# Loads and stores of a grouped softmax on two rings, the stores issued by ScalarE three tiles behind the loads

## The chip, the cores and the metric

The kernel runs on one core of a Trainium2 chip. The metric is device time in microseconds (us) of one execution. All runs that are compared here were with a granted clock of 1.0. A core has 16 transfer engines, which move all data between HBM (the large memory, where input and output lie) and SBUF (the memory that the compute engines work in). Of the compute engines this kernel needs VectorE (DVE in the profile) and ScalarE (ACT). SyncE (SP) and ScalarE can each issue transfers into a queue of their own; such a queue is called a ring here.

## The reference

```python
def reference(x):                      # x: 4 x 4096 x 4352, float32
    B, N, D = x.shape
    x_g = x.reshape(B, N, 8, D // 8)   # softmax over groups of 544
    x_g = x_g - x_g.max(axis=-1, keepdims=True)
    exp = np.exp(x_g)
    out = exp / exp.sum(axis=-1, keepdims=True)
    return out.reshape(B, N, D)
```

285 MB go in and 285 MB come out, and the arithmetic on an element is short.

## The kernel before

A tile has 256 rows of the input, two on each of 128 partitions: 34,816 bytes per partition, 4.456 MB. There are 64 tiles and six buffers. VectorE takes the negated maximum of a row, ScalarE the exponential with that maximum as bias (and the sum on the way), VectorE the reciprocal and the scaling in place. SyncE issues every transfer in one fixed order, on one ring:

```python
    with nc.Block(no_gpsimd_drain=True) as block:      # inner block
        @block.sync
        def _(sync):
            def load(t):
                b = t % NT                             # NT = 6 buffers
                if t >= NT:
                    sync.wait_ge(stored[b], 16 * (t // NT))
                sync.dma_start(out=bufs[b][:, :], in_=xt[t]).then_inc(landed[b], 16)
            for t in range(NT - 1):
                load(t)
            for t in range(nt):                        # nt = 64 tiles
                sync.wait_ge(scaled, R * (t + 1))      # R = 2 rows a tile
                sync.dma_start(out=ot[t], in_=bufs[t % NT][:, :]).then_inc(stored[t % NT], 16)
                if t + NT - 1 < nt:
                    load(t + NT - 1)
            # ... waits for the last stores
        # ... VectorE and ScalarE: hardware loops over 12 rows, VectorE one maximum ahead
```

Of the kernel before, what the change touches and what calls it, by code (L numbers as in the profile page):

```python
# [1 line left out]

# [5 lines left out]


@with_exitstack  # L10
def kernel(
    ctx: ExitStack,
    tc: tile.TileContext,
    x: bass.AP,
    out: bass.AP,
):
    nc = tc.nc
    G = 8
    P = 128
    R = 2  # L20
    NT = 6
    S = R * NT
    xf = x.flatten_outer_dims()
    of = out.flatten_outer_dims()
    N, D = xf.shape
    Dg = D // G
    nt = N // (P * R)
    nr = nt * R
    turns = (nr - 1) // S
    f32 = mybir.dt.float32  # L30
    X = mybir.AxisListType.X
    Exp = mybir.ActivationFunctionType.Exp
    xt = xf.rearrange("(t p r) d -> t p (r d)", p=P, r=R)
    ot = of.rearrange("(t p r) d -> t p (r d)", p=P, r=R)

    ctx.enter_context(tc.tile_critical(no_gpsimd_drain=True))  # L36
    ctx.enter_context(nc.cleanup_on_exit())
    bufs = [ctx.enter_context(nc.sbuf_tensor(f"xt{b}", [P, R * D], f32)) for b in range(NT)]
    mx = ctx.enter_context(nc.sbuf_tensor("mx", [P, S, G], f32))
    sm = ctx.enter_context(nc.sbuf_tensor("sm", [P, S, G], f32))  # L40
    rs = ctx.enter_context(nc.sbuf_tensor("rs", [P, S, G], f32))
    landed = [nc.alloc_semaphore(f"landed{b}") for b in range(NT)]
    stored = [nc.alloc_semaphore(f"stored{b}") for b in range(NT)]
    max_done = nc.alloc_semaphore("max_done")
    exp_done = nc.alloc_semaphore("exp_done")
    rec_done = nc.alloc_semaphore("rec_done")
    scaled = nc.alloc_semaphore("scaled")

    def row(s):
        b, r = divmod(s, R)  # L50
        return bufs[b][:, r * D:(r + 1) * D].rearrange("p (g d) -> p g d", g=G)

    def vector_max(s):
        if s % R == 0:
            nc.vector.sem_inc(landed[s // R], -16).wait_op(landed[s // R], 16, "sem-ge")  # L55
        nc.vector.reduce_max(out=mx[:, s, :], in_=row(s), axis=X, negate=True).then_inc(max_done, 1)  # L56

    def vector_scale(s):
        nc.vector.sem_inc(exp_done, -1).wait_op(exp_done, 1, "sem-ge")  # L59
        nc.vector.reciprocal(out=rs[:, s, :], in_=sm[:, s, :]).then_inc(rec_done, 1)  # L60
        nc.vector.sem_inc(rec_done, -1).wait_op(rec_done, 1, "sem-ge")  # L61
        xr = row(s)
        for g in range(G):
            i = nc.vector.tensor_scalar_mul(  # L64
                out=xr[:, g, :], in0=xr[:, g, :], scalar1=rs[:, s, g:g + 1])
        i.then_inc(scaled, 1)

    def scalar_exp(s):
        nc.scalar.sem_inc(max_done, -1).wait_op(max_done, 1, "sem-ge")  # L69
        xr = row(s)  # L70
        for g in range(G):
            i = nc.scalar.activation(  # L72
                out=xr[:, g, :],
                in_=xr[:, g, :],
                func=Exp,
                bias=mx[:, s, g:g + 1],
                scale=1.0,
                accum_out=sm[:, s, g:g + 1],
            )
        i.then_inc(exp_done, 1)  # L80

    def loop(engine):

        return nc.Fori(
            0, turns, engines=OrderedEngineSet([engine.engine]), head_slot={engine.engine: 0})

    with nc.Block(no_gpsimd_drain=True) as block:  # L87


        @block.sync  # L90
        def _(sync):
            def load(t):
                b = t % NT
                if t >= NT:
                    sync.wait_ge(stored[b], 16 * (t // NT))
                sync.dma_start(out=bufs[b][:, :], in_=xt[t]).then_inc(landed[b], 16)

            for t in range(NT - 1):
                load(t)
            for t in range(nt):  # L100
                sync.wait_ge(scaled, R * (t + 1))
                sync.dma_start(out=ot[t], in_=bufs[t % NT][:, :]).then_inc(stored[t % NT], 16)
                if t + NT - 1 < nt:
                    load(t + NT - 1)
            for b in range(NT):
                sync.wait_ge(stored[b], 16 * ((nt - b + NT - 1) // NT))


        @block.vector
        def _(vector):  # L110
            vector_max(0)
            with loop(vector):
                for s in range(S):
                    vector_max((s + 1) % S)
                    vector_scale(s)
            for n in range(turns * S, nr):
                if n + 1 < nr:
                    vector_max((n + 1) % S)
                vector_scale(n % S)

        @block.scalar
        def _(scalar):
            scalar.preload_act_table(Exp)  # L123
            with loop(scalar):
                for s in range(S):
                    scalar_exp(s)
            for n in range(turns * S, nr):
                scalar_exp(n % S)


# [1 line left out]
_INS = ['x']  # L132
_OUTS = [((4, 4096, 4352), 'float32')]


# [23 lines left out]
```

## Time and profile before

| | before |
|---|---|
| time, median (range, runs) | 1330.49 us (1329.97 to 1331.25, 4) |
| span in the trace | 1328.7 us |
| VectorE, ScalarE busy | 78%, 58% |
| bytes, mean rate over the span | 570.5 MB, 429 GB/s |
| last landing of a store, from the start | 1326.24 us |
| from there to the end of the span | 2.47 us |

The rows to start from are those of the transfers: a kernel whose 16 transfer engines are full in 39 of 40 slices has little to win elsewhere. The prediction below shows these rows and how they were read. Two more stretches of the kernel before are needed later. The columns of the row of a stretch are: stretch and its length, busy time of VectorE, ScalarE and GpSimd with the number of instructions, the granted clock, the busy share of the transfer engines, and GB/s.

```profile
64.00:66.00 2.00, 2.00 (x1) 0.68 (x2) 0.00 (x0) 1.00 1.21 522
66.00:76.00 10.00, 9.70 (x14) 6.76 (x19) 0.00 (x0) 1.00 1.00 428
76.00:80.00 4.00, 4.00 (x8) 4.00 (x12) 0.00 (x0) 1.00 1.01 435
80.00:100.00 20.00, 19.61 (x22) 13.16 (x37) 0.00 (x0) 1.00 0.98 422
...
1290.00:1300.00 10.00, 5.14 (x13) 3.99 (x12) 0.00 (x0) 1.00 1.02 439
```

There is no gap while the pipeline fills (a packet, here one row of 34,816 bytes, counts wholly where it starts, so that a short stretch can show more than 1.00), and none at 1290 to 1300 us, where the changed kernel will show one.

### The profile page before, as it was taken

What the parts mean: (1) busy time and instruction counts of PE and PEld (TensorE: products, weight loads), DVE (VectorE), ACT (ScalarE), POOL (GpSimd) and SP (SyncE); (2) the same over time, 40 slices, a digit from 0 to 9 for tenths busy, and PEclk for the clock granted to TensorE, in tenths of its full rate; (3) what the DMA queues carried; (4) which work ended last, traced back from release to release, by engine and by line L of the source; (5) the groups of instructions that cost most, each with busy time, mean ns of one, the idle gap of its engine ahead of it and who ended that gap; (6) DMA issues with size and microseconds to landing.
All of it is one profiled execution on the core that took longest, in us unless ns stands there. A gap on an engine that the chain in (4) does not pass through costs nothing. (4 is left out here: it accounts for less than half of the span.)

```text
span 1328.7 us, 4036 instructions
## 1 busy us (share of the span) xinstructions
DVE 1041.5 (78%) x1280; ACT 764.4 (58%) x2049; POOL 0.2 (0%) x4
## 2 busy tenths in 40 slices
DVE  5999987787877878778778787787877877878770
ACT  3777765655656556555565565655655556556560
POOL 0000000000000000000000000000000000000000
DMA  9999999999999999999999999999999999999997
GB/s 401 418 434 434 434 430 428 432 436 433 435 433 431 429 436 434 436 435 430 429 436 434 435 435 432 428 435 435 434 436 434 429 431 436 434 435 434 431 430 336
DMA packets 18441, 570.51 MB, mean 429 GB/s; under 512 B 2048, under 2 KB 2048, under 8 KB 2048
## 3 DMA queue, kind: packets, MB, share of 16 engines
q1 hardware_dynamic: 18432, 570.43, 99.6%
q14 instruction: 9, 0.07, 0.0%
HBM read 285.21 MB, written 285.21 MB: 429 GB/s over the span
## 5 line engine op out<-in xcount | busy, mean ns | idle before, releaser
L72 ACT ACTIVATE xt<-xt,mx 128x544 f32<-128x544 f32 x1024 | 751.3, 735 | 528.7 <-ACTq L69 528.7
L56 DVE TENSOR_REDUCE mx<-xt 128x8 f32<-128x4352 f32 x128 | 599.1, 4680 | 234.0 <-DVEq L55 233.1
L64 DVE TENSOR_SCALAR xt<-xt,rs 128x544 f32<-128x544 f32 x1024 | 434.0, 497 | 19.2 <-DVEq L61 0.9
L72 ACT ACTIVATION_READ_ACCUMULATOR xt<-xt,mx 128x1 f32 x1024 | 191.1, 187 | 0.0
L60 DVE RECIPROCAL rs<-sm 128x8 f32<-128x8 f32 x128 | 24.5, 191 | 3.2 <-DVEq L59 3.2
L123 ACT ACT_TABLE_LOAD x1 | 1.3, 1283 | 0.9 <-SPq L36 0.9
L143 POOL MEMSET const-bfloat16-1.0<- 128x1 bf16 x1 | 0.1, 102 | 0.0
L143 POOL MEMSET const-uint8-127<- 128x1 uint8 x1 | 0.1, 102 | 0.0
L143 POOL MEMSET const-float32-0.0<- 128x1 f32 x1 | 0.1, 99 | 0.2 <-issue 0.2
L143 POOL MEMSET const-float32-1.0<- 128x1 f32 x1 | 0.1, 99 | 0.0
## 6 DMA issues: line engine op xcount, KB each, us to landing
xt<-in_x_dram SPq DMA_DIRECT2D x64, 4352.0 KB, 30.8
out_dram<-xt SPq DMA_DIRECT2D x64, 4352.0 KB, 40.7
```

The source lines that it names most:

```text
L56: nc.vector.reduce_max(out=mx[:, s, :], in_=row(s), axis=X, negate=True).then_inc(max_done, 1)
L60: nc.vector.reciprocal(out=rs[:, s, :], in_=sm[:, s, :]).then_inc(rec_done, 1)
L64: i = nc.vector.tensor_scalar_mul(out=xr[:, g, :], in0=xr[:, g, :], scalar1=rs[:, s, g:g + 1])
L72: i = nc.scalar.activation(out=xr[:, g, :], in_=xr[:, g, :], func=Exp, bias=mx[:, s, g:g + 1], scale=1.0, accum_out=sm[:, s, g:g + 1],)
L123: scalar.preload_act_table(Exp)
L143: nc = _bacc.Bacc("TRN2", target_bir_lowering=False, num_devices=1)
```

## The change

Its intent: give loads and stores a ring each, so that neither is stuck behind the other in one queue; take the issue of stores from SyncE to ScalarE, inside its hardware loop; keep the distance steady by issuing the store of tile t only when the load of tile t + 3 has been seen; and drop the inner block with its barrier and cleanup.

```diff
+    LAG = 3
-    ctx.enter_context(nc.cleanup_on_exit())
...
+    def store(b, target):
+        take(nc.scalar, scaled, R)
+        nc.scalar.dma_start(out=target, in_=bufs[b][:, :]).then_inc(stored[b], 16)
+    def scalar_tile(j, target=None):
+        take(nc.scalar, seen)            # VectorE adds 1 when load j has landed
+        if target is not None:
+            store((j - LAG) % NT, target)
+        for r in range(R):
+            scalar_exp(j * R + r)
-    with nc.Block(no_gpsimd_drain=True) as block:
...
+    for t in range(nt):                  # SyncE: loads only
+        b = t % NT
+        if t >= NT:
+            nc.sync.wait_ge(stored[b], 16 * (t // NT))
+        nc.sync.dma_start(out=bufs[b][:, :], in_=xt[t]).then_inc(landed[b], 16)
...
+    for j in range(LAG):
+        scalar_tile(j)
+    with loop(nc.scalar) as u:
+        for b in range(NT):
+            scalar_tile(LAG + b, turn_out[u, b])
+    for j in range(rest, nt):
+        scalar_tile(j, ot[j - LAG])
+    for t in range(nt - LAG, nt):
+        store(t % NT, ot[t])
```

(`take` waits for a semaphore and counts it down. The arithmetic on both engines is unchanged.)

More of the change, by code (lines that the diff above doesn't have):

```diff
@@ L27 @@
     nt = N // (P * R)
-    nr = nt * R
-    turns = (nr - 1) // S
+    turns = (nt - LAG) // NT
+    rest = LAG + turns * NT
     f32 = mybir.dt.float32
@@ L34 @@
     ot = of.rearrange("(t p r) d -> t p (r d)", p=P, r=R)
+    turn_out = of[:turns * S * P, :].rearrange("(u b p r) d -> u b p (r d)", b=NT, p=P, r=R)
+    landed = [tc.alloc_semaphore(f"landed{b}") for b in range(NT)]
+    stored = [tc.alloc_semaphore(f"stored{b}") for b in range(NT)]
+    seen = tc.alloc_semaphore("seen")
+    max_done = tc.alloc_semaphore("max_done")
+    exp_done = tc.alloc_semaphore("exp_done")
+    rec_done = tc.alloc_semaphore("rec_done")
+    scaled = tc.alloc_semaphore("scaled")
     ctx.enter_context(tc.tile_critical(no_gpsimd_drain=True))
-    ctx.enter_context(nc.cleanup_on_exit())
     bufs = [ctx.enter_context(nc.sbuf_tensor(f"xt{b}", [P, R * D], f32)) for b in range(NT)]
@@ L41, with loop, take @@
     rs = ctx.enter_context(nc.sbuf_tensor("rs", [P, S, G], f32))
-    landed = [nc.alloc_semaphore(f"landed{b}") for b in range(NT)]
-    stored = [nc.alloc_semaphore(f"stored{b}") for b in range(NT)]
-    max_done = nc.alloc_semaphore("max_done")
-    exp_done = nc.alloc_semaphore("exp_done")
-    rec_done = nc.alloc_semaphore("rec_done")
-    scaled = nc.alloc_semaphore("scaled")
+    def loop(engine):
+        return nc.Fori(
+            0, turns, engines=OrderedEngineSet([engine.engine]), head_slot={engine.engine: 0})
+    def take(engine, sem, n=1):
+        engine.sem_inc(sem, -n).wait_op(sem, n, "sem-ge")
     def row(s):
@@ L51, in row, with vector_max, vector_scale @@
         return bufs[b][:, r * D:(r + 1) * D].rearrange("p (g d) -> p g d", g=G)
-    def vector_max(s):
+    def vector_max(n):
+        s = n % S
         if s % R == 0:
-            nc.vector.sem_inc(landed[s // R], -16).wait_op(landed[s // R], 16, "sem-ge")
+            take(nc.vector, landed[s // R], 16)
+            nc.vector.sem_inc(seen, 1)
         nc.vector.reduce_max(out=mx[:, s, :], in_=row(s), axis=X, negate=True).then_inc(max_done, 1)
-    def vector_scale(s):
-        nc.vector.sem_inc(exp_done, -1).wait_op(exp_done, 1, "sem-ge")
+    def vector_scale(n):
+        s = n % S
+        take(nc.vector, exp_done)
         nc.vector.reciprocal(out=rs[:, s, :], in_=sm[:, s, :]).then_inc(rec_done, 1)
-        nc.vector.sem_inc(rec_done, -1).wait_op(rec_done, 1, "sem-ge")
+        take(nc.vector, rec_done)
         xr = row(s)
@@ L66, in vector_scale, with scalar_exp @@
         i.then_inc(scaled, 1)
-    def scalar_exp(s):
-        nc.scalar.sem_inc(max_done, -1).wait_op(max_done, 1, "sem-ge")
+    def scalar_exp(n):
+        s = n % S
+        take(nc.scalar, max_done)
         xr = row(s)
@@ L80, in scalar_exp @@
         i.then_inc(exp_done, 1)
-    def loop(engine):
-        return nc.Fori(
-            0, turns, engines=OrderedEngineSet([engine.engine]), head_slot={engine.engine: 0})
-    with nc.Block(no_gpsimd_drain=True) as block:
-        @block.sync
-        def _(sync):
-            def load(t):
-                b = t % NT
-                if t >= NT:
-                    sync.wait_ge(stored[b], 16 * (t // NT))
-                sync.dma_start(out=bufs[b][:, :], in_=xt[t]).then_inc(landed[b], 16)
-            for t in range(NT - 1):
-                load(t)
-            for t in range(nt):
-                sync.wait_ge(scaled, R * (t + 1))
-                sync.dma_start(out=ot[t], in_=bufs[t % NT][:, :]).then_inc(stored[t % NT], 16)
-                if t + NT - 1 < nt:
-                    load(t + NT - 1)
-            for b in range(NT):
-                sync.wait_ge(stored[b], 16 * ((nt - b + NT - 1) // NT))
-        @block.vector
-        def _(vector):
-            vector_max(0)
-            with loop(vector):
-                for s in range(S):
-                    vector_max((s + 1) % S)
-                    vector_scale(s)
-            for n in range(turns * S, nr):
-                if n + 1 < nr:
-                    vector_max((n + 1) % S)
-                vector_scale(n % S)
-        @block.scalar
-        def _(scalar):
-            scalar.preload_act_table(Exp)
-            with loop(scalar):
-                for s in range(S):
-                    scalar_exp(s)
-            for n in range(turns * S, nr):
-                scalar_exp(n % S)
@@ new lines, with vector_rows @@
+    for b in range(NT):
+        nc.sync.wait_ge(stored[b], 16 * ((nt - b + NT - 1) // NT))
+    nc.scalar.preload_act_table(Exp)
+    for j in range(LAG):
+        scalar_tile(j)
+    with loop(nc.scalar) as u:
+        for b in range(NT):
+            scalar_tile(LAG + b, turn_out[u, b])
[3 more added lines that the diff above has]
+        store(t % NT, ot[t])
+    def vector_rows(lo, hi):
+        for n in range(lo, hi):
+            vector_max(n + 1)
+            vector_scale(n)
@@ L132 @@
+    vector_max(0)
+    vector_rows(0, LAG * R)
+    with loop(nc.vector):
+        vector_rows(LAG * R, LAG * R + S)
+    vector_rows(rest * R, nt * R - 1)
+    vector_scale(nt * R - 1)
 _INS = ['x']
```

## The prediction

> **What bounds the kernel now.** I read the page from its top: the busy shares, then the two rows of transfers in the slices, then the queue.
>
> ```profile
> DVE 1041.5 (78%) x1280; ACT 764.4 (58%) x2049; POOL 0.2 (0%) x4
> ...
> DMA  9999999999999999999999999999999999999997
> GB/s 401 418 434 434 434 430 428 432 436 433 435 433 431 429 436 434 436 435 430 429 436 434 435 435 432 428 435 435 434 436 434 429 431 436 434 435 434 431 430 336
> ...
> q1 hardware_dynamic: 18432, 570.43, 99.6%
> ```
>
> No compute engine is full: VectorE works 78% of the span, ScalarE 58%. The 16 transfer engines are full from the first slice to the last but one, and one queue holds all of it: 64 loads and 64 stores of 4.456 MB. So the transfers are the bound, and the next view is who waits in the queue of SyncE.
>
> ```profile
> SPq L96 <- DMA out_dram<-xt: 1141.2, 58, 20.7
> SPq L102 <- DVE xt L64: 102.4, 6, 33.3
> SPq L106 <- DMA out_dram<-xt: 28.0, 1, 28.0
> ```
>
> Line 96 is the load. All 58 loads that reuse a buffer wait for the store that frees it, up to 20.7 us each, which is one load and one store. A store waits for its scaling on VectorE only six times in 64. The stretches give the rate inside, and at both ends (the last column is GB/s, the one before it the busy share of the transfer engines):
>
> ```profile
> 0.00:5.00 5.00, 0.00 (x0) 1.28 (x1) 0.20 (x4) 1.00 0.65 224
> 5.00:10.00 5.00, 0.00 (x0) 0.00 (x0) 0.00 (x0) 1.00 1.02 440
> 640.00:1140.00 500.00, 396.98 (x491) 290.38 (x779) 0.00 (x0) 1.00 1.00 433
> 1310.00:1320.00 10.00, 0.00 (x0) 0.00 (x0) 0.00 (x0) 1.00 0.95 411
> 1320.00:1328.70 8.70, 0.00 (x0) 0.00 (x0) 0.00 (x0) 1.00 0.15 65
> ```
>
> In the middle 500 us hold 433 GB/s, so a tile takes 4.456 / 0.433 = 10.3 us each way, and all 570.43 MB take 1317.4 us. The span is 1328.7. The 11.3 us over it lie at the ends: at the start 224 of 440 GB/s over 5 us, so the stream flows at about 2.45 us (the first issue is at 0.95: **1.5 us from issue to flow**); at the end 65 GB/s over 8.7 us is 0.57 MB, 16 rows of 34,816 bytes, on the few transfer engines that lag while the others are done; SyncE then passes its last wait at 1326.26 and spends 2.4 us on the exit. A change can win only from these 11 us, from the 1.5 us between the span and the timed 1330.2, or from a higher rate.
>
> **What the Trainium skill says.** "DMA: Bandwidth & Descriptors", section "Issuing engines are not separate DMA queues": transfers issued by different engines run on the same 16 transfer engines and interleave, and issuing from more than one saves only issue time. The trace agrees as far as it goes: 99.6% of 16 engines' span is taken by one queue, and nothing waits for issue. The same page, "Queues, rings and completion order": a transfer engine takes turns between the queues that have work, a packet at a time. No run here shows it yet, since there is one queue; from it I take that a load and a store in flight together get half the rate each. The same page, "Where 436 GB/s comes from": a ceiling of 435.2 GB/s. The trace's 433 is 99.5% of it. The same page, "Latency and other measured facts": copies through the sync and scalar queues at 214 GB/s per direction, 428 in sum, with rows of 16 KiB. That is the only figure for two directions at once; the trace's alternation on one ring has 433, so mixing would cost 1.2% if the figure carried over to rows of 34 KB. I doubt that it does in full.
>
> **Part by part.** *(1) Bytes and arithmetic.* Unchanged: 64 loads, 64 stores, 128 maxima of 4.68 us, 1024 exponentials of 0.735, 1024 scalings of 0.497. Change of the floor: 0.
>
> *(2) Two rings instead of one.* In the steady state the load ring has the next load or two, and the store ring one or two stores, so neither the engines nor their rate changes: a load and a store side by side take 20.6 us together, as one after the other do now. At 433 GB/s: 0. If 428: 1.2% of 1317, +15 us. If 435.2: -6.6 us.
>
> *(3) Filling.* Now SyncE issues store 0 at 37.53 us, as tile 0 is scaled, behind five loads, and the engines stay full. In the changed kernel ScalarE issues store 0 in its own order: after the exponentials of tiles 0 to 2 and after load 3 has been seen. In the filling it makes a tile in 16.5 us (two rows of 8.24, the distance of the maxima at 45.66 and 53.91, which VectorE sets with 4.68 + 0.19 + 3.39); the exponentials of tile 2 end at 64.7 us, in the timeline of ScalarE:
>
> ```profile
> 64.49 0.19 ACT L72 ACTIVATION_READ_ACCUMULATOR xt<-xt,mx 128x1 f32 x1
> 66.96 0.75 ACT L72 ACTIVATE xt<-xt,mx 128x544 f32<-128x544 f32 x1 [2.28 <-ACTq L69]
> ```
>
> (the end of row 5, start and duration ahead; then the first of row 6). Store 0 then flows at 64.7 + 1.5 = 66.2. The six loads, all issued at once now, are through at 2.45 + 6 x 10.3 = 64.3 and the seventh needs store 0's buffer. **Idle: 1.9 us.** Store 0 alone runs to 76.5; load 6 is issued on its landing and flows some 2 us later (1.5 plus a short landing, an estimate), while store 1 comes only at 64.7 + 16.5 + 1.5 = 82.7. **Idle: 2 us.** From then on the pair wants 20.6 us of every 16.5 that ScalarE could serve, so the engines fill up and stay so. Transfer engines that lag catch up in these gaps, so I count 2 to 4 us, not the whole 3.9: +3.
>
> *(4) Draining.* Now the last tile's arithmetic is hidden: behind the last load stand five stores (51 us), and VectorE is done some 23 us after it lands. After the change four to five stores still stand behind it, but ScalarE issues only store 60 at the landing, then does the exponentials of tile 63 (from 14.59 to 31.2 for tile 0: 16.6 us), and only then issues stores 61, 62 and 63. Store 61 flows 18.1 us after the landing. Until then the engines have store 60 (10.3 us) and what is left of store 59. If that is 7.8 us there is no gap; if it is nothing the gap is about 6. Because ScalarE began late (part 3), stores lag behind and much is left: +0 to 6, I take +1.5.
>
> *(5) Ends of the program.* The inner block with its barrier and the cleanup fall away. In the trace SyncE leaves its last wait at 1326.46, the block's barrier is over at 1326.85, the cleanup at 1327.35: -0.9 us. The start gains 0.1 at most.
>
> *(6) Issue on ScalarE.* 64 issues of 0.33 to 0.43 us are 25 us on an engine that is idle for 529 us, and 64 more semaphore steps on VectorE: both beside the transfers, 0 on the end.
>
> Sum: 1330.2 + 3 + 1.5 - 0.9 = 1333.8; a third of a chance each way for the rate to be a little lower or higher leaves it near there. I say **1333**.
>
> **The rivals.** *Rate down:* loads and stores mixed on each transfer engine cost turnarounds. For it: the 428 above, and the early slices of the page, where the rate is a little less even than later. Against: in the kernel before, every engine turns from loads to stores each 10.3 us, and the stretch of 640 to 1140 us holds 433. It would make 1340 to 1350. *Rate up:* two rings hide the gap between packets, or reads and writes go beside each other. Against: 433 is within 0.5% of the stated ceiling, and the transfer shares in the page are full. It would make 1325 at best; over 2% would need 443 GB/s. *ScalarE becomes the bound:* it waits for stores' tiles in order, so a late scaling would hold up exponentials, and then buffers. Against: 11.9 us busy per 20.6 us, and the tile that it stores is two tiles older than the one that it works on; the scaling is long done. *Hidden anyway:* the gaps of parts 3 and 4 don't arise because lagging engines fill them; then only the exit counts, 1329.
>
> **Range and chances.** Low: the exit gained, no gap, the rate near the ceiling: 1323. High: both gaps in full and most of the 1.2%: 1346. Two per cent faster is 1303.6, below the 1317.4 that the bytes take at 433, so it needs a rate never seen here: 2%. Two per cent slower is 1356.8: a rate of about 424 or less, 5%. Within: 93%.
>
> **What would show each step.** Two queues with 285 MB each and a sum of the rate near 433 in the middle (part 2); a load issued every 20.6 us. The first store issue near 64.7 us on ScalarE, and stretches at 64 to 66 and 76 to 79 us well under 433 (part 3). A dent some 12 to 18 us after the last load has landed, and the last three stores issued together at its end (part 4). About 1.5 us instead of 2.4 from the last wait to the end of the span (part 5). Idle of ScalarE about as before (part 6). The prediction is wrong if the rate in the middle is under 428 or over 436, or if one of the rings runs dry in the steady state, seen as slices under 9 or as waits of ScalarE for scaled tiles.

## The result, and the profile after

| | before | after |
|---|---|---|
| time, median (range, runs) | 1330.49 us (1329.97 to 1331.25, 4) | 1333.93 us (1333.79 to 1334.07, 4) |
| ratio, 95% interval | | 1.0025 (1.0008 to 1.0043) |
| last landing of a store | 1326.24 us | 1330.49 us |
| from there to the end of the span | 2.47 us | 1.68 us |

Ratios here are the mean time of one kernel's fast runs over that of the other's of the same rounds, so they are not quite the ratios of the medians quoted beside them. The change made the kernel 3.4 us slower, a quarter of a per cent, and the interval leaves out 1. By the mark of 2% it is the same. The prediction said 1333.

The page of the changed kernel, in the rows that answer to those that the prediction shows of before:

```profile
DVE 1041.5 (78%) x1280; ACT 764.4 (57%) x2049; POOL 0.2 (0%) x4
...
DMA  9999999999999999999999999999999999999988
GB/s 401 417 400 425 433 431 433 434 433 433 433 432 433 435 435 434 432 433 435 432 433 433 433 433 435 434 434 433 433 434 432 434 433 432 433 435 435 434 373 386
...
q1 hardware_dynamic: 9216, 285.22, 49.7%
q10 hardware_dynamic: 9216, 285.22, 49.7%
```

Two queues now hold half each. The middle slices are as before, 433 GB/s. What differs is the third slice (400 against 434) and the last but one (373 against 430), while the very last is fuller (386 against 336). The waits of SyncE:

```profile
SPq L114 <- DMA out_dram<-xt: 1230.8, 58, 74.5
SPq L116 <- DMA out_dram<-xt: 75.9, 1, 75.9
```

A load still waits for the store that frees its buffer, 58 times; the longest wait is now 74.5 us, for store 0. ScalarE, in the waits of all engines:

```profile
ACT xt L87 <- ACTq L58: 536.7, 127, 16.6
```

It is idle for about as long as before (529 us). The stretches of the changed kernel (columns as above):

```profile
64.00:66.00 2.00, 2.00 (x1) 0.04 (x1) 0.00 (x0) 1.00 0.07 22
66.00:76.00 10.00, 9.70 (x16) 7.36 (x20) 0.00 (x0) 1.00 1.04 443
76.00:80.00 4.00, 4.00 (x7) 4.00 (x13) 0.00 (x0) 1.00 0.82 348
80.00:100.00 20.00, 19.55 (x24) 13.16 (x36) 0.00 (x0) 1.00 1.02 404
640.00:1140.00 500.00, 392.52 (x481) 286.61 (x770) 0.00 (x0) 1.00 1.00 433
...
1290.00:1300.00 10.00, 9.40 (x14) 7.71 (x22) 0.00 (x0) 1.00 0.67 286
```

There is a gap at 64 to 66 us, a second at 76 to 80, then 404 GB/s where the kernel before has 422; the middle is unchanged; and there is a dent of about (433 - 286) / 433 x 10 = 3.4 us at 1290 to 1300.

To add these up I took the records of the packets themselves: the mean over the 16 transfer engines of the time in which no row is in flight, and the sum of the times of the rows. The last row ends at 1325.91 us before and at 1330.02 after, 4.11 later. Of that, 2.92 us is more idle time (8.01 against 5.09), and 1.21 is longer rows (their times sum to 1323.02 us per engine against 1321.81), 4.13 together. The idle time itself has moved: the filling has some 2.3 us that it had not, the drain 4.7 (1260 to 1300 us), and the last six microseconds, in which most of the 16 engines of the kernel before are done and wait for a few that lag, have lost 3.9.

That last point leaves a doubt. A mean over 16 engines says what all of them lost; the end is set by the slowest one. The trace does not name the transfer engine of a packet, but it has 16 increments of the semaphore for every transfer (2048 for 128). I take each for one engine whose share has landed, so that the spread of the 16 shows how far the slowest lags. Around the end of the changed kernel:

```
transfer    first of 16 lands   9th, 15th, 16th behind the first (us)
load 62         1256.7 us           0.9  1.3  5.3
load 63         1277.4              0.9  1.3  5.3
store 60        1294.6              0.1  0.9  5.0
store 61        1309.3              0.1  0.2  0.7
```

One engine lands 4 to 5 us behind the other fifteen until the dent, and within 0.7 us of the first after it. For this one engine the dent at 1290 to 1300 us was hardly there: it was still busy with store 60. So two theories stood against each other:

- **The mean gap counts.** Filling and draining both cost what their gaps measure.
- **The slowest engine counts.** Only what this engine sees of a gap costs anything, so the filling gap costs (all engines stand still) and the drain gap does not.

A third was that two rings cost something all along and the ends do not matter.

### The profile page after: what moved, and what is told of

Read it like the earlier page. It is cut to its first block, busy times and chain, and to the rows that moved or that the text cites. A ratio compares the mean times of both kernels' runs of the same rounds, so it can differ in the third digit from the quotient of the medians.

```text
span 1332.2 us, 4328 instructions
## 1 busy us (share of the span) xinstructions
DVE 1041.5 (78%) x1280; ACT 764.4 (57%) x2049; POOL 0.2 (0%) x4
## 2 busy tenths in 40 slices
DMA packets 18439, 570.49 MB, mean 428 GB/s; under 512 B 2048, under 2 KB 2048, under 8 KB 2048
```

## The experiments

Twelve runs, in four groups, each group on one chip with its own runs of the kernel before (median of before in the groups: 1330.96, 1331.27, 1331.31 and 1330.48 us). All gave the right result. Each edit below is against the changed kernel, unless it says otherwise, and shows the main lines (`...` marks a cut).

**The block alone (e1_no_block).** The order of issue of the kernel before, on one ring, but built like the changed kernel, without the inner block and cleanup (here in short and against the kernel before):

```diff
-    with nc.Block(no_gpsimd_drain=True) as block:  # and cleanup_on_exit()
+    # the same loads and stores on nc.sync, straight in the body
```

> The order of issue of the kernel before on one ring; only the inner block, its barrier and the cleanup are gone. If the exit is worth what the two traces show (2.45 us from the last landing to the end of the span before, 1.67 after), 1329.7 us against 1330.5. If the block is worth nothing of its own: 1330.5.

Measured: 1329.91 us, ratio 0.9988 (0.9975 to 1.0002); before 1330.96. From the last landing to the end of the span it takes 1.49 us instead of 2.47. The trace shows the gain; in the times it is just inside the noise.

**The drain gap (e2_drain).** Store 61 goes with store 60, and store 62 between the two rows of the last tile:

```diff
-    for j in range(rest, nt):
+    for j in range(rest, nt - 1):
         scalar_tile(j, ot[j - LAG])
-    for t in range(nt - LAG, nt):
-        store(t % NT, ot[t])
+    take(nc.scalar, seen)
+    store((nt - 4) % NT, ot[nt - 4])
+    store((nt - 3) % NT, ot[nt - 3])
+    scalar_exp(nt * R - 2)
+    store((nt - 2) % NT, ot[nt - 2])
+    scalar_exp(nt * R - 1)
+    store((nt - 1) % NT, ot[nt - 1])
```

> The changed kernel, but at its end store 61 is issued with store 60 and store 62 between the two rows of tile 63, so that nothing waits behind the exponentials. Theory 'the mean gap counts' (the drain gap of 4.7 us, mean over the 16 transfer engines, is lost time): 1329 to 1330 us against 1333.9. Rival 'the slowest transfer engine counts' (in the trace of the changed kernel one engine lands 5 us behind the others and has no gap there, so the gap costs nothing): 1333.2 to 1333.9.

Measured: 1334.5 us, ratio 1.0024 (1.0011 to 1.0038), against 1.0025 of the changed kernel. Nothing was won, though the gap is gone:

```profile
1290.00:1300.00 10.00, 8.64 (x12) 7.72 (x22) 0.00 (x0) 1.00 0.94 401
1300.00:1310.00 10.00, 3.59 (x9) 1.23 (x4) 0.00 (x0) 1.00 1.02 439
1310.00:1320.00 10.00, 0.00 (x0) 0.00 (x0) 0.00 (x0) 1.00 1.03 446
1320.00:1326.00 6.00, 0.00 (x0) 0.00 (x0) 0.00 (x0) 1.00 0.67 290
1326.00:1331.00 5.00, 0.00 (x0) 0.00 (x0) 0.00 (x0) 1.00 0.05 21
```

The last stretch tells why. In it 21 GB/s move, 0.1 MB in 5 us, three rows one after the other at 1.29 us each: a single transfer engine at work. The last row ends at 1330.57 us, where it ended at 1330.02 with the gap. The increments say the same: those of store 63 begin 5.0 us earlier than with the gap (1324.9 us instead of 1329.9), but the last of them comes at 1331.0 instead of 1330.5. And in the changed kernel itself the last increments of stores 60 to 63 come at 1299.6, 1310.0, 1320.2 and 1330.5 us, one every 10.3 us, so that the slowest engine sees no gap there; in the kernel before they come at 1295.4 to 1326.2. The whole 4.2 us are lost before store 60 has landed. The theory of the mean gap falls.

**The filling gap (e3_lag2, and again as e3b_lag2).** One number changes. At a distance of two tiles store 0 waits for the exponentials of tiles 0 and 1 only:

```diff
-    LAG = 3
+    LAG = 2
```

> The changed kernel with a distance of two tiles instead of three: store 0 is issued after the exponentials of tile 1, near 48 us, while loads still run. Theory 'the filling gap counts' (about 2.2 us idle at 65 to 67 and 76 to 78 us, and some slow packets after it): 1330.5 to 1332 us against 1333.9. Rival 'two rings cost something all along, the ends do not matter': 1333.9, no change.

> Distance two once more, for comparison in the same rounds: 1330.2 by all theories.

Measured: 1330.16 and 1330.15 us, ratios 0.9991 (0.9977 to 1.0004) and 0.9993 (0.9979 to 1.0006). This is the whole loss: from 1.0025 to about 0.9992 is 1.0033, some 4.3 us. The gaps of the filling are gone (e3b_lag2), but so is the one of the drain (0.03 us idle at 1260 to 1300 us, instead of 4.7), so that this run alone doesn't tell the two apart; e2_drain and e6_first do.

```profile
64.00:66.00 2.00, 2.00 (x4) 2.00 (x7) 0.00 (x0) 1.00 1.21 522
66.00:76.00 10.00, 9.85 (x11) 7.37 (x20) 0.00 (x0) 1.00 1.02 439
76.00:80.00 4.00, 3.85 (x7) 2.07 (x5) 0.00 (x0) 1.00 0.99 426
80.00:100.00 20.00, 19.70 (x25) 15.43 (x43) 0.00 (x0) 1.00 0.98 423
```

With two rings, distance two and no block it is as fast as e1_no_block with one ring: two rings as such neither gain nor lose, within the noise of 0.13%.

**Two queues without ScalarE (e5_pool).** The stores are issued by GpSimd, each as soon as its tile is scaled:

```diff
-        nc.scalar.dma_start(out=target, in_=bufs[b][:, :]).then_inc(stored[b], 16)
...
+    for t in range(nt):
+        take(nc.gpsimd, scaled, R)
+        nc.gpsimd.dma_start(out=ot[t], in_=bufs[t % NT][:, :]).then_inc(stored[t % NT], 16)
```

> Loads from SyncE, stores from GpSimd's own queue, each as soon as its tile is scaled: two queues in the steady state, but no store behind exponentials, so no gap at either end; no block. Theory 'only the order at the ends costs': like e1_no_block, 1329 to 1331 us. Rival 'two queues side by side cost in the steady state': 1333 or more, and a rate in the middle under 433 GB/s.

Measured: 1333.91 us, ratio 1.0021 (1.0007 to 1.0035). By its time alone the rival would have won. The trace says otherwise: the middle holds 433 GB/s (the third busy time, 12.78, is GpSimd's), and the last store lands at 1325.56 us, earlier than in the kernel before.

```profile
640.00:1140.00 500.00, 393.99 (x488) 291.30 (x783) 12.78 (x24) 1.00 1.00 433
```

The span then goes on for 6.58 us, because a drain of GpSimd takes 5.29 us at the exit. So my number for this run was wrong, through a cost of the experiment itself, and its transfers agree with e3_lag2: two queues cost nothing in the steady state.

**The filling gap made larger (e4_lag4).**

```diff
-    LAG = 3
+    LAG = 4
-    turns = (nt - LAG) // NT
+    turns = (nt - LAG - 1) // NT
```

(The second edit only leaves the last six tiles to the code after the loop, which needs them.)

> The changed kernel with a distance of four tiles: store 0 waits behind the exponentials of tile 3, near 81.5 us, while the six loads are through at 65. Theory 'the filling gap is what costs': about 17 us idle there instead of 2, and more idle after it while ScalarE serves a store each 16.5 us: 1348 to 1358 us against 1333.9. Rival 'the filling does not matter': 1334, no change.

Measured: 1388.27 us, ratio 1.0425 (1.0409 to 1.0441), 30 us more than the top of what I expected (the trace is of the slowest of its four runs, 1392.14 us).

```profile
64.00:66.00 2.00, 2.00 (x1) 0.01 (x1) 0.00 (x0) 1.00 0.04 17
66.00:82.00 16.00, 15.70 (x21) 11.93 (x32) 0.00 (x0) 1.00 0.17 70
82.00:100.00 18.00, 17.55 (x24) 12.61 (x34) 0.00 (x0) 1.00 0.89 341
640.00:1140.00 500.00, 381.38 (x468) 278.89 (x749) 0.00 (x0) 1.00 1.00 420
```

The filling behaves as expected: 17.6 us idle between 64 and 100 us, some 15 more than in the changed kernel. But the steady state, which I had taken to be untouched, falls to 420 GB/s. The last row ends 58.3 us later than in the changed kernel; 22.5 of it is idle time, and 35.8 is longer rows. Between 200 and 1200 us, 811 rows take over 1.4 us (1.83 on average, instead of 1.29), where the changed kernel has none. Slow rows of this kind also stand in the changed kernel at 76 to 100 us, after its second gap, and in the kernel before around its first store (1.44 us on average at 50 to 60 us). Why distance four has so many I did not test.

**Store 0 alone (e6_first, and again as e6b_first).** Distance two could also win in the steady state. So here the distance stays three, and only store 0 moves ahead of the exponentials of tile 2; tile 3 then carries no store:

```diff
-    for j in range(LAG):
-        scalar_tile(j)
+    scalar_tile(0)
+    scalar_tile(1)
+    take(nc.scalar, seen)
+    store(0, ot[0])
+    scalar_exp(4)
+    scalar_exp(5)
+    scalar_tile(3)               # the loop starts at tile 4 with store 1
...
```

> The changed kernel, distance three from tile 4 on, but store 0 alone is moved ahead of the exponentials of tile 2 (issued near 48 us as in e3_lag2), and no store goes with tile 3. Theory 'the filling gap costs': most of what e3_lag2 won, 1330 to 1331.5 us against 1333.9. Rival 'e3_lag2 won by the shorter distance in the steady state': 1333.5 to 1334.5.

> Store 0 alone moved, once more in the same rounds: 1331.6 us by all theories.

Measured: 1331.57 and 1331.31 us, ratios 1.0002 (0.9989 to 1.0016) and 1.0003 (0.9990 to 1.0017). One store, moved by a tile of arithmetic, wins 0.22%, about 3 us of the 4.3. (It was issued at 43.5 us rather than near 48; its first row starts at 51 to 52 us, where it does so at 58.2 in e3b_lag2 and at 66.5 in the changed kernel.) The two profiled runs of this kernel came out at 1332.05 and 1330.13 us; the first has slow rows when load 6 starts near 76 us (0.98 us on the average engine), the second 0.02. The remaining microsecond against distance two is within that scatter. So the rival, the shorter distance in the steady state, is left with no more than that.

**Both ends (e7_lag2_drain, e8_first_drain), and the changed kernel again (e0_after).** The new end of e2_drain, put on e3_lag2 and on e6_first:

```diff
-    LAG = 3
+    LAG = 2                      # e7; e8 has the filling of e6_first
+    # both: the end of e2_drain
```

> Distance two and the end reordered, store 62 between the two rows of tile 63: the best of the parts together. Theory 'the slowest transfer engine sets the end': 1330.2, as e3_lag2, since no gap is left that this engine sees. Rival 'what is left of the drain gap still counts': 1328.5 to 1329.5.

> Store 0 moved and the end reordered as in e2_drain, the distance still three. The trace of e6_first has a mean gap of 5.9 us at the end, and the engine that lagged by 6.5 us before it lags by 0.2 after it, so there some 1.5 to 2 us of the gap are seen by the slowest engine. Theory 'a gap costs what the slowest engine sees of it': 1329.5 to 1330.3 us, though the same reordering gave nothing in e2_drain. Rival 'the drain gap never costs anything': 1331.6, as e6_first.

> The changed kernel itself, for comparison in the same rounds: 1334 us by all theories.

Measured: e7_lag2_drain 1330.05 us, 0.9992 (0.9978 to 1.0006); e8_first_drain 1331.14 us, 1.0000 (0.9986 to 1.0013); e0_after 1334.08 us, 1.0023 (1.0009 to 1.0036). So reordering the end gave nothing beyond the noise on three different fillings, of which the third had no drain gap to begin with:

| | end as changed | end reordered |
|---|---|---|
| filling as changed | 1.0025, 1.0023 | 1.0024 |
| store 0 moved | 1.0002, 1.0003 | 1.0000 |
| distance two | 0.9991, 0.9993 | 0.9992 |

My expectation for e8_first_drain, that part of the drain gap would show there, did not come true. It was too large: the last increments of stores 60 and 61 lie 11.1 us apart in the profiled run of e6_first, 0.8 more than a transfer takes, and 10.3 apart in that of e6b_first, and the noise hides the rest. e7_lag2_drain shows best what the end hangs on, since no gap is left in it. Here are the loads into the third buffer, every twelfth transfer, and how far (us) the last increments come behind the first:

```
first lands   390.1  513.5  636.9  760.3  883.7  1007.1  1130.5  1253.9
15th behind     1.3    1.3    1.3    1.3    1.3     1.3     1.3     1.3
16th behind     1.4    2.0    2.7    3.3    3.9     4.5     5.1     5.8
```

Here the last increment falls back by 0.6 us in every 123, and the fifteenth not at all: one transfer engine, as I read it, is slower than the rest. The changed kernel has the same rate from 391 to 885 us (2.4, 3.1, 3.7, 4.3, 4.9), but then its lag stands still at 5.2 to 5.3; in the kernel before it stands at 5.9 from 508 us on, and there four engines lag by 3.5 to 6 us. So neither the rate nor the one engine is a rule. A lagging engine must still move its 1024 rows, and the kernel ends with it. Which engine it is, why it is slow and why its lag stops growing, the trace doesn't tell.

**The first issue of ScalarE (e9_warm).** One line of the trace did not fit my working: the first store's issue, in the timeline of ScalarE of the changed kernel:

```profile
60.55 5.44 ACTq L99 DMA_DIRECT2D out_dram<-xt  x1
...
63.85 0.19 ACT L87 ACTIVATION_READ_ACCUMULATOR xt<-xt,mx 128x1 f32 x1
66.36 0.75 ACT L87 ACTIVATE xt<-xt,mx 128x544 f32<-128x544 f32 x1 [2.33 <-ACTq L58]
```

It starts while the exponentials of tile 2 still run, so the issuing queue is ahead of the arithmetic here; and it takes 5.44 us, where the median of all 64 is 0.34. (In e4_lag4, where the loads are through by then, the first one takes 1.96.) Perhaps this delayed store 0, and not the order. A small load at the very start uses the ring once:

```diff
+    nc.scalar.dma_start(out=warm[:, :], in_=xt[0][:, :G]).then_inc(warmed, 16)
...
```

> The changed kernel, with one small load (128 rows of 32 bytes, never read) issued by ScalarE at the start, ahead of its first store. In the traces the first issue of ScalarE takes 5.0 to 5.5 us (60.55 to 66.0) where every later one takes 0.34. Theory 'the first issue on a ring that was never used is what delays store 0': the small load takes the delay, store 0 is issued in some 0.35 us near 60.6, the gap at 64 to 66 us is gone and the time is 1331.5 to 1332.7 us against 1334. Rival 'store 0 is late because of ScalarE's order alone, or the long issue has another cause': the issue still takes 5 us, or the gap stays, and the time is 1334.

Measured: 1333.65 us, ratio 1.0023 (1.0010 to 1.0037). Here half of each theory came true. The issue is short and the gap at 64 to 66 us nearly gone, but the time has not moved beyond the noise. (The trace is of the fastest of the five runs, 1332.48 us; the others took 1333.63 to 1334.12.)

```profile
60.78 0.37 ACTq L101 DMA_DIRECT2D out_dram<-xt  x1
```

```profile
64.00:66.00 2.00, 2.00 (x1) 0.26 (x2) 0.00 (x0) 1.00 0.70 296
66.00:76.00 10.00, 9.70 (x15) 7.14 (x19) 0.00 (x0) 1.00 0.92 394
76.00:80.00 4.00, 4.00 (x7) 4.00 (x13) 0.00 (x0) 1.00 0.66 279
```

The idle time moved to 70 to 82 us (1.9 us there). That makes sense: until store 1 flows at 77.5 us, which ScalarE's pace of 16.5 us a tile decides, all the work there is are six loads and store 0, 7 x 10.3 = 72.1 us from 2.45 on, so 74.6; and load 6 can't start before store 0 has landed. Whether store 0 flows at 65 or at 66.5, the engines run dry before 77. Moving it by a whole tile (e6_first) lets load 6 start soon enough to close the gap: it is issued at 73.2 us there, and its first row starts at 75.5.

No run beats the kernel before beyond the noise. The best are e1_no_block (0.9988) and the kernels of distance two (0.9991 to 0.9993), and the intervals of all of them reach past 1. The transfer engines are full in these, and what is left at the end is the one that lags, or the few (in e1_no_block four shares of the last store land 4.4 to 6.4 us behind its first).

## Why the prediction was right

It said 1333 us and the runs showed 1333.93. By its own steps:

1. **Bytes and arithmetic: 0.** Right; busy times are the same to 0.1%.
2. **Two rings: 0.** Right. The middle holds 433 GB/s in both kernels, and e3_lag2 on two rings equals e1_no_block on one. The 428 for mixed directions (an estimate: twice the 214 that the Trainium skill gives for one direction), which I doubted but left room for in the range, did not show. The taking of turns, which I had from the skill and no run had shown, is in the trace: with two rings in the middle of the run the rows of one transfer spread over 21.8 us, with one ring over 11.5, so that a load and a store in flight do share the engines.
3. **Filling: +3.** Right in kind. Store 0 alone (e6_first) is worth 3 us; distance two wins 4.3, and takes the drain gap away with it. The first gap was as said: 1.8 us idle at 64 to 70 us, where 1.9 was said. The second came at its place, but was shorter, 0.5 us instead of 2, and ended in another way. Load 6 did not end it: issued at 78.35 us, it had its first row at 83.08, 4.7 us later and not 2. Store 1 did: it was issued at 76.49, before the exponentials of tile 3 had ended, and had its first row at 77.33, where 82.7 was said. What it left out are the slow rows after the second gap, seen as 404 against 422 GB/s at 80 to 100 us. On the mean engine the idle time of the filling is 2.3 us longer and the rows of the first 200 us are 1.2 us longer in sum; the 0.8 us that are left of the 4.3 I can't place. One number came out right through two errors: store 0 flows at 66.5 us where 66.2 was said, but its issue began at 60.55, ahead of the exponentials and not behind them, and took 5.4 us instead of the 0.3 to 0.4 that I had taken from SyncE. e9_warm shows that this hardly matters.
4. **Draining: +1.5.** Wrong in both its halves; this is the step that failed. The gap is larger than I took it (4.7 us on the mean engine, within the 0 to 6 said), since fifteen engines had next to nothing of store 59 left (it landed on them by 1284.8 us) when the last load had landed (1282.7), where I argued for a backlog. It ended otherwise too: stores 61 and 62 were issued at 1297.69 and 1298.16 us, before the exponentials of tile 63 end at 1302.0, and only store 63 came after them, at 1305.98. And the gap costs nothing, since the sixteenth engine does not see it. That gaps may be filled by lagging engines stood among the rivals; it came true at the end and not in the filling.
5. **Ends of the program: -0.9.** Right: 1.68 us instead of 2.47 after the last landing, -0.8.
6. **Issue on ScalarE: 0.** Right: it is idle for 537 us, as against 529.

The measured parts are 4.3 + 0 - 0.8 = 3.5 us (the first from times, the last from traces); measured in all is 3.4. The sum of 3 + 1.5 - 0.9 = 3.6 hit it by luck: the term for the drain, which should have been 0, stood in for what the filling had been given too little. That the change is a small loss, set by the filling and the exit at an unchanged rate, was no luck. One side figure is slightly off: by the prediction's own terms 2% faster would need about 442 GB/s, not 443; nothing rests on it.

## What to carry to other kernels

Here the transfers ran at 433 GB/s with one ring and with two: a second ring moved no more bytes. What a new order of issue could still do was lose time where the pipeline fills, because an engine that issues stores in order between its own arithmetic frees the first buffer only when it has come through the tiles ahead. Count, for the first tiles, what work the transfer engines have until that first store flows. And before you close a gap that the mean rate shows, look whether the slowest of the 16 engines sees it too: here 4.7 us of idle time in the drain were free, and 2.3 us in the filling cost 3 to 4.3, together with what followed them.

## What the Trainium skill lacked or had wrong

- "DMA: Bandwidth & Descriptors", section "Latency and other measured facts", has 214 GB/s per direction for copies between HBM tensors on the sync and scalar queues (tiles of 128 partitions by 16 KiB, padded row pitch); it has no figure for loads and stores of SBUF side by side. With rows of 34,816 bytes the sum of both directions here is 433 GB/s, the same on one ring and on two.
- The same section says that transfer engines 7 and 15 are usually slower and ties this, as a guess, to descriptors written by software. In e7_lag2_drain and the changed kernel both data queues are of the hardware kind, and still one share of 16 falls behind by 0.6 us in every 123 us for long stretches, as shown above; in the first the end of the kernel is set by it. Which engine it is, the trace doesn't show.
- No page that I read has the cost of a first issue on ScalarE's ring while loads run: 3.3 to 5.5 us in the traces (1.96 in e4_lag4, with the loads through), against a median of 0.34. In e9_warm, where a small load went first at the start, the first store's issue took 0.37.
- No page that I read says how long a transfer on one ring waits for the other: in e9_warm the issue of store 0 ended at 61.15 us and its first row started at 65.01, 3.9 us later, with loads still under way; for load 6 of the changed kernel, behind store 1, it was 4.4 us (78.68 to 83.08); with idle engines (store 0 of the changed kernel) 0.5 us.
- No page that I read has the slow rows: 1.83 us on average instead of 1.29 for 811 rows of e4_lag4 between 200 and 1200 us. The cause is open.
- No page that I read has the drain of GpSimd at the exit of a kernel whose stores it issued: 5.29 us in e5_pool.
